# Gate and up products of one request group in Strassen's way, in a two-group FFN on one core

## The chip, the cores and the metric

The kernel runs on one core of one Trainium2 chip, as one launch. The metric is the device time of a run in microseconds (us); lower is better. Three runs of the kernel before gave 1458.1, 1460.4 and 1462.01 us, so the median is 1460.4 us.

The engines are called by the profile's names: PE multiplies matrices (PEld loads its weights), DVE and POOL do element-wise work, ACT evaluates functions and copies, and SP issues the transfers. Each engine works through its own queue in order. PE writes its sums to the PSUM banks; the other operands lie in SBUF.

## The reference, cut to what matters

One encoder layer is computed for a prompt of 1024 frames and a sample of 32 frames, with the same weights. A mixing half (three kinds of heads, an output projection and a first norm) comes first. The change lies in the second half, the feed-forward part, with 1024 model columns and 2816 hidden ones:

```
h = x * (1 + sc2) + sh2
y = (jax.nn.silu(h @ w_gate) * (h @ w_up)) @ w_down
x = _layer_norm(ALPHA * x + (1 + g2) * y, ln2_g, ln2_b)
```

All inputs and outputs are float32.

## The kernel before, in words

**Layout and precision.** Activations are held transposed: 128 model columns on the partitions, frames along the row. The 1056 frames are two groups: group 0 is the first 512 frames, group 1 the other 544 (512 of the prompt and the 32 of the sample). Each group is cut in two column ranges (`MM`, L27), for group 1 of 272 frames each. A float32 operand is split in two parts that PE takes at full rate: a rounded `hi` (ACT, L102 for weights) and the rest `lo` = x - hi (DVE, L103). `gemm` (L108 to L116) makes each product of three matmuls: hi by hi (L114), hi by lo (L115), lo by hi (L116). With 8 blocks of 128 model columns, one product of a 128-column weight tile with one column range is 24 matmuls.

**Weights.** `weights` (L91) loads 128x1024 values (512 KB) into a buffer `raw` (3 of them, `RAW`), and splits them into `whi` and `wlo` (3 of each, `WB`). `w_gu` holds the 1024x128 gate tile and the 1024x128 up tile of hidden tile j as units 2j and 2j+1.

**up** (L965 to L983) makes one tile of 128 hidden units for one group: for each column range a gate product into a PSUM bank of pool `pg` and an up product into one of pool `pu` (3 banks each for group 1), silu as three ACT activations (exp, ln, exp, L977 to L979), two DVE multiplications (L980, L981), and a split into `acth` (ACT, L982) and `actl` (DVE, L983), of which 5 tiles are kept. One tile of group 1 is 4 products or 96 matmuls.

**down** (L999) multiplies 3 or 4 such tiles (`GROUPS`, L29) with `w_down` and adds the result to the residual `z` from PSUM (DVE, L918, in `sublayer_end`). For group 1 the order is: up tiles 0 to 3, down of tiles 0 to 2, up 4 to 6, down, up 7 to 10, down, up 11 to 14, down, up 15 to 18, down. Each `down` stands behind the up of the first tile of the next set. Tiles 19 to 21, their down and group 1's second norm end the kernel (L1218 to L1234).

**Second norm of group 0.** `ln2` (L1013) takes the sums over `z` of group 0 that POOL and DVE made during the last down of group 0 (L835, L844 to L847, L915), makes mean and variance with PE (L854, L856), and then scales and shifts 8 blocks in each of two column ranges: DVE multiplies (L1021), DVE or POOL adds (L1022, "vpvvpvvp": three of eight on POOL), ACT applies gain and bias (L1024), and SP stores to `o_yT`. It is emitted behind up tiles 0 to 3 of group 1 (L1213 to L1215).

**What sets the order.** The program is written with a tile framework. It allots each tile a buffer of its pool and tag, makes an instruction wait until the buffer's last readers are done, and orders each engine's queue by a list schedule in which the place in the program is the priority. The buffers of `z` of group 0 (16 KB on each partition, tag `z0` of pool `pz`) come free when `ln2` of group 0 has been stored; those of the operand of group 0 (`ah0`, `ah256`, `al0`, `al256` of pool `ph`) when its last up tile is done.

The loop in question, before:

```
for g, (j0, nj) in enumerate(GROUPS[:-1]):
    for j in range(j0 + (g > 0), j0 + nj + 1):
        self.up(1, j, act, pa, MM[1])
    if g == 0:
        for a, b in LN[0]:
            self.ln2(0, st, a, b, "vpvvpvvp", "aaaaaaaa")
    st = self.ln_begin(nc.gpsimd, sum=False) if g == last - 1 else None
    self.down(1, g, act, MM[1], st)
```

Of the kernel before, what the change touches and what calls it, by code (L numbers as in the profile page):

```python
# [7 lines left out]
F32 = mybir.dt.float32  # L8
F32R = mybir.dt.float32r
AF = mybir.ActivationFunctionType  # L10
ALU = mybir.AluOpType
# [4 lines left out]
P = 128  # L16
D = 1024
KT = 8
S = 1024
T = 1056  # L20
# [4 lines left out]
GN = (512, 544)  # L25
QD = 2
MM = (((0, 256), (256, 512)), ((0, 272), (272, 544)))  # L27
LN = MM
# [17 lines left out]
FP = (0, 0)  # L46
RAW = 3
WB = 3
ALPHA = 2.0 ** 0.25
LN_EPS = 1e-5  # L50
HN_EPS = 1e-6
# [12 lines left out]
def f(ap):  # L64
    return ap.bitcast(F32)


class Kernel:
# [22 lines left out]
    def weights(self, src, nk, ncol, eng=None):  # L91
# [4 lines left out]
        for k0 in range(0, nk, step):  # L96
            w = step * ncol
            raw = self.t(self.wp, [P, 1056], F32, "raw", RAW)
            self.load(raw[:, :w], src[:, k0 * ncol:k0 * ncol + w])
            hi = self.t(self.wp, [P, 1056], F32R, "whi", WB)  # L100
            lo = self.t(self.wp, [P, 1056], F32R, "wlo", WB)
            nc.scalar.copy(hi[:, :w], raw[:, :w])  # L102
# [16 lines left out]
    def constants(self):  # L119
# [68 lines left out]
    def ada_end(self, u, po):  # L188
# [776 lines left out]
    def up(self, c, j, act, pool, cuts):  # L965
        self.phase = f"up{c}"
        nc, hh, hl = self.nc, self.hh[c], self.hl[c]
        ah, al = act[j] = [self.t(pool, [P, GN[c]], F32R, x, 5) for x in ("acth", "actl")]
        w = [self.weights(self.d["w_gu"][2 * j + i], KT, P) for i in range(2)]
        for a, b in cuts:  # L970
            ps = []
            for i in range(2):
                p = self.t((self.pg, self.pu)[i], [P, 512], F32, self.utag[i])[:, :b - a]
                self.gemm(p, w[i], slice(0, P), lambda k: hh[a][:, k], lambda k: hl[a][:, k])
                ps.append(p)
            s = self.t(self.p2, [P, 272], F32, "sil", 4)[:, :b - a]
            nc.scalar.activation(s, ps[0], AF.Exp, scale=-1.0)  # L977
            nc.scalar.activation(s, s, AF.Ln, bias=self.one)
            nc.scalar.activation(s, s, AF.Exp, scale=-1.0)  # L979
            nc.vector.tensor_tensor(s, ps[0], s, ALU.mult)  # L980
            nc.vector.tensor_tensor(s, ps[1], s, ALU.mult)  # L981
            nc.scalar.copy(ah[:, a:b], s)  # L982
            nc.vector.tensor_tensor(al[:, a:b], s, f(ah[:, a:b]), ALU.subtract)  # L983

    def last_weights(self, dst, units):

        nc = self.nc
        j0, nj = GROUPS[-1]
        w = nj * 256
        out = {}  # L990
        for i, (hi, lo) in zip(units, dst):
            raw = self.t(self.wp, [P, 1056], F32, "raw", RAW)
            self.load(raw[:, :w], self.d["w_dn"][i][:, j0 * 256:(j0 + nj) * 256])
            nc.scalar.copy(hi, raw[:, :w])
            (nc.gpsimd if LWE else nc.vector).tensor_tensor(lo, raw[:, :w], f(hi), ALU.subtract)
            out[i] = [(hi[:, k * 256:(k + 1) * 256], lo[:, k * 256:(k + 1) * 256]) for k in range(nj)]
        return out
# [43 lines left out]
    def run(self):  # L1041
        nc, tc, d = self.nc, self.tc, self.d
        dr = self.pool("dr", space=DRAM)
        t = lambda shape, tag: self.t(dr, shape, F32, tag)
# [14 lines left out]
        s3 = ExitStack()  # L1059
# [15 lines left out]
        w2, w3 = d["w_in"], d["w_in_f"]  # L1075
# [88 lines left out]
        st = self.ln_begin(nc.gpsimd)  # L1164
# [14 lines left out]
        pa = self.pool("pa0", ctx=s5)  # L1179
        self.pu, self.utag = self.pg, "gg"  # L1180
        act = {}
# [27 lines left out]
        act = {}  # L1209
        for g, (j0, nj) in enumerate(GROUPS[:-1]):  # L1210
# [128 lines left out]
```

## Time and profile before

| what | us |
|---|---|
| median of 3 runs | 1460.4 |
| lowest and highest run | 1458.1, 1462.01 |
| the profiled execution | 1461.59 |
| its span, first to last instruction | 1459.8 |
| PE busy, PEld busy | 1396.7, 1345.1 |
| DVE busy, ACT busy, POOL busy | 964.8, 627.2, 283.8 |

The profiled execution is one run of its own; 1.8 us of it lie outside the span. Its tables give, for a group of like instructions, the source line, the engine, the operation, `out<-in` by tile names and shapes, the count, the busy time and the mean of one in ns, and behind the bar the time that the engine stood idle ahead of them and who ended that. Tile names keep the phase in which the buffer was first named, so `wo_ah` is the FFN operand of group 1, `wo_z` its residual and `mlstm_z` that of group 0. Times in windows and timelines count from the start of the span. Group 1's up tiles begin at about 1040 us.

### The profile page before, as it was taken

How to read it: one execution, taken by the hardware profiler on the slowest of the kernel's cores; microseconds unless marked ns; L12 is line 12 of the kernel's file. 1: busy time of each engine (PE TensorE's matmuls, PEld its weight loads, DVE VectorE, ACT ScalarE, POOL GpSimd, SP SyncE). 2: the span in 40 equal slices, each digit the busy share in tenths (PEclk: the TensorE clock that was granted, in tenths of full speed). 3: DMA queues.
4: the chain of work that ended last, by engine and by line, in shares of the span. 5: the costliest groups of instructions: out<-in, count | busy, mean ns of one | idle time of the engine just before them, and what ended most of it. 6: DMA issues, size and time to landing. Idle time of an engine off the chain costs nothing.

```text
span 1459.8 us, 28886 instructions
## 1 busy us (share of the span) xinstructions
PE 1396.7 (96%) x11141; PEld 1345.1 (92%) x11141; DVE 964.8 (66%) x2220; ACT 627.2 (43%) x1365; POOL 283.8 (19%) x335
## 2 busy tenths in 40 slices
PE   7999999999999899999999998998999999999995
PEld 4899988989898799999999998998999999999994
DVE  5558655678698677787877755677648545454676
ACT  3223244534453454555454542334445342424353
POOL 0104100143187300000000000647601000000433
PEclk9999999999999999999999998999999999999997
DMA  9754768563754755444433535321224322222331
GB/s 361 260 194 126 221 199 243 194 197 121 250 188 144 204 166 151 126 125 139 130 111 108 101 94 136 109 86 59 87 73 137 110 87 87 88 88 87 124 108 62
DMA packets 120865, 207.33 MB, mean 142 GB/s; under 512 B 21380, under 2 KB 76300, under 8 KB 120728
## 3 DMA queue, kind: packets, MB, share of 16 engines
q1 hardware_dynamic: 120728, 205.49, 44.8%
q8 instruction: 88, 1.44, 0.4%
q14 instruction: 49, 0.40, 0.1%
HBM read 173.78 MB, written 31.66 MB: 141 GB/s over the span
## 4 chain that ended last, share of the span: by engine, by line
PE 80%; DMA 6%; DVE 6%; POOL 3%; issue 2%; ACT 1%; SPq 1%; DVEq 0%; ACTq 0%; POOLq 0%
PE up_g L115 7%; PE up_g L116 7%; PE up_g L114 7%; PE dn_g L114 4%; PE dn_g L115 4%; PE dn_g L116 4%; PE up_u L116 3%; PE up_u L115 3%; PE up_u L114 3%; PE tm_g L279 3%; PE tm_g L280 3%; PE tm_g L281 3%; PE fox_t L729 2%; PE wo_g L116 2%; PE wo_g L115 2%
## 5 line engine op out<-in xcount | busy, mean ns | idle before, releaser
L114 PE MATMUL up_g<-wo_ah,up_whi 128*128 128x256 f32 (+1 forms) x1056 | 304.1, 289 | 13.2 <-DVE up_sil L980 5.6
L115 PE MATMUL up_g<-wo_al,up_whi 128*128 128x256 f32 (+1 forms) x1056 | 305.3, 289 | 0.1
L116 PE MATMUL up_g<-wo_ah,up_wlo 128*128 128x256 f32 (+1 forms) x1056 | 304.6, 289 | 0.0
L114 PEld LDWEIGHTS up_g<-wo_ah,up_whi 128*128 128x128 f32 x1056 | 201.9, 191 | 16.5 <-DVE up_sil L980 6.0
L115 PEld LDWEIGHTS up_g<-wo_al,up_whi 128*128 128x128 f32 x1056 | 202.1, 191 | 1.4 <-DVE wo_al L938 0.7
L116 PEld LDWEIGHTS up_g<-wo_ah,up_wlo 128*128 128x128 f32 x1056 | 201.7, 191 | 0.7 <-DVE up_wlo L103 0.4
L103 DVE TENSOR_TENSOR up_wlo<-up_raw,up_whi 128x1024 fp32r<-128x1024 f32 x94 | 120.8, 1285 | 68.5 <-ACT up_whi L102 68.2
L102 ACT CAST up_whi<-up_raw 128x1024 fp32r<-128x1024 f32 x94 | 98.5, 1048 | 142.3 <-PE dn_u L115 53.9
L114 PE MATMUL dn_g<-up_acth,dn_whi 128*128 128x256 f32 (+1 forms) x496 | 146.7, 296 | 9.5 <-DVE mlstm_z L918 6.4
L115 PE MATMUL dn_g<-up_actl,dn_whi 128*128 128x256 f32 (+1 forms) x496 | 144.4, 291 | 0.0
L116 PE MATMUL dn_g<-up_acth,dn_wlo 128*128 128x256 f32 (+1 forms) x496 | 143.8, 290 | 0.0
L280 PE MATMUL tm_g<-tm_wlo,start_h1h 128*128 128x256 f32 (+1 forms) x384 | 110.8, 289 | 0.0
L281 PE MATMUL tm_g<-tm_whi,start_h1l 128*128 128x256 f32 (+1 forms) x384 | 110.4, 288 | 0.0
L279 PE MATMUL tm_g<-tm_whi,start_h1h 128*128 128x256 f32 (+1 forms) x384 | 109.8, 287 | 0.2 <-ACT tm_mixs L630 0.2
L114 PE MATMUL fm_g<-start_h1h,fm_whi 128*128 128x256 f32 (+2 forms) x344 | 102.0, 302 | 6.1 <-DVE fm_qkl L364 2.2
L114 PEld LDWEIGHTS dn_g<-up_acth,dn_whi 128*128 128x128 f32 x496 | 96.7, 195 | 11.5 <-DVE mlstm_z L918 7.5
L115 PE MATMUL fm_g<-start_h1l,fm_whi 128*128 128x256 f32 (+2 forms) x344 | 101.8, 296 | 0.2 <-DVE start_h1l L220 0.2
L116 PE MATMUL up_u<-wo_ah,up_wlo 128*128 128x272 f32 x352 | 101.9, 290 | 0.0
L114 PE MATMUL up_u<-wo_ah,up_whi 128*128 128x272 f32 x352 | 101.2, 288 | 0.0
L115 PE MATMUL up_u<-wo_al,up_whi 128*128 128x272 f32 x352 | 101.0, 287 | 0.0
L116 PE MATMUL fm_g<-start_h1h,fm_wlo 128*128 128x256 f32 (+2 forms) x344 | 100.8, 294 | 0.0
L115 PEld LDWEIGHTS dn_g<-up_actl,dn_whi 128*128 128x128 f32 x496 | 96.9, 195 | 0.3
(458 smaller groups left out, 3758.9 us busy)
## 6 DMA issues: line engine op xcount, KB each, us to landing
up_raw<-w_gu SPq DMA_DIRECT2D x94, 512.0 KB
dn_raw<-w_dn SPq DMA_DIRECT2D x30, 512.0 KB
ada_late<-w_ada SPq DMA_DIRECT2D x24, 512.0 KB
wo_raw<-w_o SPq DMA_DIRECT2D x24, 512.0 KB
ada_araw<-w_ada SPq DMA_DIRECT2D x16, 512.0 KB
fm_raw<-w_in_f SPq DMA_DIRECT2D x16, 512.0 KB
tm_raw<-w_in SPq DMA_DIRECT2D x12, 512.0 KB
dn_raw<-w_dn SPq DMA_DIRECT2D x16, 384.0 KB
```

The lines of the kernel that those rows point to most:

```text
L102: nc.scalar.copy(hi[:, :w], raw[:, :w])
L103: (eng or nc.vector).tensor_tensor(lo[:, :w], raw[:, :w], f(hi[:, :w]), ALU.subtract)
L114: nc.tensor.matmul(ps, hi, xh(k), start=start and k == 0, stop=False)
L115: nc.tensor.matmul(ps, hi, xl(k), start=False, stop=False)
L116: nc.tensor.matmul(ps, lo, xh(k), start=False, stop=stop and k == n - 1)
L279: nc.tensor.matmul(ps[:, :ncol], xh, hi, start=k == 0, stop=False)
L280: nc.tensor.matmul(ps[:, :ncol], xh, lo, start=False, stop=False)
L281: nc.tensor.matmul(ps[:, :ncol], xl, hi, start=False, stop=k == 7)
L729: nc.tensor.transpose(ps[:, y * P:(y + 1) * P], probs[y][:, b * P:(b + 1) * P], self.ident)
```

## The change

Tiles 5 to 18 of group 1 (`SJ = 5`; 14 of 22) are made by a new function `sup` in place of `up`. Tiles 0 to 4 and 19 to 21 stay. A tile's four products form a 2x2 block problem: the weight is cut in gate and up, and along the model columns in a lower and an upper half of 4 blocks each; the operand is cut in its two column ranges and the same halves. That is eight block products of 12 matmuls; Strassen's scheme in Winograd's form makes them from seven:

- `sup_operand`, emitted behind tile 2, makes four combinations T of the operand blocks on POOL, 10 additions or subtractions of 128x272 for each of 4 blocks, and splits each into hi and lo (ACT copy, DVE subtraction). They take the buffers of group 0's operand.
- `sup` makes four combinations of each tile's weights on POOL (128x512 each, three of them in place in the raw buffers), and splits 1024 + 1024 + 512 + 1024 columns in place of 1024 + 1024. `w3` has one buffer and `w4` two, all in the memory of group 0's `z0` (`sup_begin`).
- The seven products go to `pu` and `pg` in turn and are added up on the way out of PSUM: two ACT copies and five DVE additions that read PSUM, two POOL additions, and the multiplication of silu on POOL. For even tiles the gate's raw weights have a buffer `sraw` of their own.

The first emission of `ln2` for group 0 moves from behind tile 3 to behind tile 1. The operand buffers are given with 272 columns for either group.

```diff
     def operand(self, c, pool):
-        self.hh[c], self.hl[c] = ({a: self.t(pool, [P, KT, b - a], F32R, f"{x}{a}", 1) for a, b in MM[c]}
-                                  for x in ("ah", "al"))
+        new = lambda tag, n: self.t(pool, [P, KT * 272], F32R, tag, 1)[:, :KT * n].rearrange("p (k n) -> p k n", k=KT)
+        self.hh[c], self.hl[c] = ({a: new(f"{x}{a}", b - a) for a, b in MM[c]} for x in ("ah", "al"))
...
+    def sup_operand(self):
...
+        eng = nc.gpsimd
+        for k in range(4):
+            b = [[(f(hh[t][:, i]), f(hl[t][:, i])) for t in (0, 272)] for i in (k, k + 4)]
+            new = lambda: self.t(self.p2, [P, 272], F32, "tmp", 4)
+            def split(i, x):
+                nc.scalar.copy(self.T[i][0][:, k], x)
+                nc.vector.tensor_tensor(self.T[i][1][:, k], x, f(self.T[i][0][:, k]), ALU.subtract)
+            def diff(x, y):
+                u, v = new(), new()
+                eng.tensor_tensor(u, x[0], y[0], ALU.subtract)
+                eng.tensor_tensor(v, x[1], y[1], ALU.subtract)
+                eng.tensor_tensor(u, u, v, ALU.add)
+                return u
+            split(0, diff(b[0][1], b[0][0]))
+            t3 = diff(b[1][1], b[0][1])
+            split(2, t3)
+            t2 = new()
+            eng.tensor_tensor(t2, t3, b[0][0][0], ALU.add)
+            eng.tensor_tensor(t2, t2, b[0][0][1], ALU.add)
+            split(1, t2)
+            t4 = new()
+            eng.tensor_tensor(t4, b[1][0][0], t2, ALU.subtract)
+            eng.tensor_tensor(t4, t4, b[1][0][1], ALU.add)
+            split(3, t4)
+    def sup_begin(self):
+        x = self.t(self.pz, [P, 4096], F32R, "z0", 1)
+        self.w3 = x[:, 0:1024], x[:, 1024:2048]
+        self.w4 = [(x[:, i:i + 512], x[:, i + 512:i + 1024]) for i in (2048, 3072)]
+    def sup(self, j, act, pool):
...
+        eng = nc.gpsimd
+        split(*w1, rg)
+        eng.tensor_tensor(s3, rg[:, lo], ru[:, lo], ALU.subtract)
+        eng.tensor_tensor(ru[:, lo], ru[:, lo], ru[:, hi], ALU.add)
+        split(*w2, ru)
+        eng.tensor_tensor(rg[:, lo], ru[:, lo], rg[:, lo], ALU.subtract)
+        eng.tensor_tensor(rg[:, hi], rg[:, hi], rg[:, lo], ALU.subtract)
+        split(*w4, s3)
+        split(*self.w3, rg)
...
+        nc.scalar.copy(u2, prod(blocks(w1, 0), own(0, 0)))
+        add(nc.vector, x0, prod(blocks(w1, 512), own(0, 4)), u2)
+        g0 = silu(x0)
+        nc.scalar.copy(c5, prod(blocks(w2, 0), com(0)))
+        add(nc.vector, u2, prod(blocks(self.w3, 0), com(1)), u2)
+        add(eng, x1, u2, c5)
+        add(nc.vector, x1, prod(blocks(self.w3, 512), own(272, 4)), x1)
+        g1 = silu(x1)
+        add(nc.vector, u3, prod(blocks(w4, 0), com(2)), u2)
+        add(eng, c5, u3, c5)
+        end(g1, c5, slice(272, 544))
+        add(nc.vector, u3, prod(blocks(w2, 512), com(3)), u3)
+        end(g0, u3, slice(0, 272))
...
             for j in range(j0 + (g > 0), j0 + nj + 1):
-                self.up(1, j, act, pa, MM[1])
-            if g == 0:
-                for a, b in LN[0]:
-                    self.ln2(0, st, a, b, "vpvvpvvp", "aaaaaaaa")
+                if j == SJ:
+                    self.sup_begin()
+                if j < SJ:
+                    self.up(1, j, act, pa, MM[1])
+                else:
+                    self.sup(j, act, pa)
+                if j == 1:
+                    for a, b in LN[0]:
+                        self.ln2(0, st, a, b, "vpvvpvvp", "aaaaaaaa")
+                if j == 2:
+                    self.sup_operand()
```

Here `silu(x)` is exp, ln, exp on ACT and a multiplication on POOL, and `end` is a DVE multiplication, an ACT copy to `acth` and a DVE subtraction to `actl`.

More of the change, by code (lines that the diff above doesn't have):

```diff
@@ L48 @@
 WB = 3
+SJ = 5
 ALPHA = 2.0 ** 0.25
@@ new lines, in sup_begin, with split, prod, silu @@
+    def sup_begin(self):
[3 more added lines that the diff above has]
+    def sup(self, j, act, pool):
+        self.phase = "sup"
+        nc = self.nc
+        hh, hl, T = self.hh[1], self.hl[1], self.T
+        ah, al = act[j] = [self.t(pool, [P, GN[1]], F32R, x, 5) for x in ("acth", "actl")]
+        if j % 2:
+            rg = self.t(self.wp, [P, 1056], F32, "raw", RAW)[:, :1024]
+        else:
+            rg = self.t(self.px, [P, 1024], F32, "sraw", 1)
+        ru = self.t(self.wp, [P, 1056], F32, "raw", RAW)[:, :1024]
+        self.load(rg, self.d["w_gu"][2 * j])
+        self.load(ru, self.d["w_gu"][2 * j + 1])
+        def split(hi, lo, x):
+            nc.scalar.copy(hi, x)
+            nc.vector.tensor_tensor(lo, x, f(hi), ALU.subtract)
+        w1, w2 = ([self.t(self.wp, [P, 1056], F32R, x, WB)[:, :1024] for x in ("whi", "wlo")] for _ in range(2))
+        lo, hi = slice(0, 512), slice(512, 1024)
+        s3 = self.t(self.px, [P, 512], F32, "s3", 1)
+        w4 = self.w4[j % 2]
+        eng = nc.gpsimd
[7 more added lines that the diff above has]
+        split(*self.w3, rg)
+        blocks = lambda w, c: [(w[0][:, c + k * P:c + k * P + P], w[1][:, c + k * P:c + k * P + P]) for k in range(4)]
+        whole = slice(0, P)
+        def prod(ps, w, x, start=True, stop=False):
+            self.gemm(ps, w, whole, *x, start=start, stop=stop)
+        own = lambda t, k0: (lambda k: hh[t][:, k0 + k], lambda k: hl[t][:, k0 + k])
+        com = lambda i: (lambda k: T[i][0][:, k], lambda k: T[i][1][:, k])
+        n = [0]
+        def prod(w, x):
+            n[0] += 1
+            ps = self.t((self.pg, self.pu)[n[0] % 2], [P, 512], F32, "gu"[n[0] % 2])[:, :272]
+            self.gemm(ps, w, whole, *x)
+            return ps
+        c = lambda p, tag: self.t(p, [P, 272], F32, tag, 4)
+        add = lambda e, o, x, y: e.tensor_tensor(o, x, y, ALU.add)
+        def silu(x):
+            s = c(self.p2, "sil")
+            nc.scalar.activation(s, x, AF.Exp, scale=-1.0)
+            nc.scalar.activation(s, s, AF.Ln, bias=self.one)
+            nc.scalar.activation(s, s, AF.Exp, scale=-1.0)
+            eng.tensor_tensor(s, x, s, ALU.mult)
+            return s
+        def end(s, x, sl):
+            nc.vector.tensor_tensor(s, x, s, ALU.mult)
+            nc.scalar.copy(ah[:, sl], s)
+            nc.vector.tensor_tensor(al[:, sl], s, f(ah[:, sl]), ALU.subtract)
+        u2 = c(self.px, "c")
+        nc.scalar.copy(u2, prod(blocks(w1, 0), own(0, 0)))
+        x0 = c(self.p2, "tmp")
+        add(nc.vector, x0, prod(blocks(w1, 512), own(0, 4)), u2)
+        g0 = silu(x0)
+        c5 = c(self.px, "c")
+        nc.scalar.copy(c5, prod(blocks(w2, 0), com(0)))
+        add(nc.vector, u2, prod(blocks(self.w3, 0), com(1)), u2)
+        x1 = c(self.p2, "tmp")
+        add(eng, x1, u2, c5)
+        add(nc.vector, x1, prod(blocks(self.w3, 512), own(272, 4)), x1)
+        g1 = silu(x1)
+        u3 = c(self.p2, "sil")
+        add(nc.vector, u3, prod(blocks(w4, 0), com(2)), u2)
[3 more added lines that the diff above has]
+        end(g0, u3, slice(0, 272))
```

9 lines of the change are left out of this document (added).

## The prediction

> **What bounds the kernel now.** I read the page first, then the windows of the stretch that the change touches.
>
> ```profile
> span 1459.8 us, 28886 instructions
> PE 1396.7 (96%) x11141; PEld 1345.1 (92%) x11141; DVE 964.8 (66%) x2220; ACT 627.2 (43%) x1365; POOL 283.8 (19%) x335
> PE 80%; DMA 6%; DVE 6%; POOL 3%; issue 2%; ACT 1%; SPq 1%; DVEq 0%; ACTq 0%; POOLq 0%
> ```
>
> ```profile
> core 0: us, PE busy (x) PEld busy (x) DVE busy (x) ACT busy (x) POOL busy (x), PEclk, DMA share, GB/s
> 1040.00:1088.00 48.00, 48.00 (x385) 47.95 (x384) 21.51 (x35) 22.18 (x42) 4.20 (x5) 1.00 0.23 69
> 1088.00:1108.00 20.00, 20.00 (x157) 19.84 (x156) 19.38 (x46) 10.79 (x20) 2.44 (x3) 1.00 0.45 153
> 1144.00:1162.00 18.00, 18.00 (x145) 18.00 (x144) 12.78 (x29) 3.95 (x6) 0.00 (x0) 1.00 0.38 136
> 1162.00:1306.00 144.00, 144.00 (x1151) 144.00 (x1151) 67.00 (x120) 51.57 (x88) 0.00 (x0) 1.00 0.27 89
> 1306.00:1354.00 48.00, 48.00 (x385) 48.00 (x385) 19.89 (x32) 21.45 (x39) 0.00 (x0) 1.00 0.24 77
> ```
>
> PE is the chain (80%), and from 1040 to 1354 it never rests, at full clock: 1306 to 1354 is four up tiles, 384 matmuls in 48.0 us, 12.0 us a tile. That is 48.0/385 = 0.1247 us a matmul. The second window holds group 0's norm and most of the first down; DVE is full there (19.38 of 20), yet PE doesn't wait. So in this stretch a matmul less is 0.125 us less, provided that the other engines still feed PE. POOL is empty from 1144 on. The end of the kernel is not touched.
>
> **The change part by part.**
>
> *Removed from PE.* Seven products of 12 matmuls for eight: 12 x 0.1247 = 1.50 us a tile, 10.5 us for 12.0, and **20.9 us** over 14 tiles.
>
> *Added elsewhere.* Durations of before, from the groups of lines of DVE and ACT (1162 to 1282) and from timelines of POOL and DVE:
>
> ```profile
> L103 DVE TENSOR_TENSOR up_wlo<-up_raw,up_whi 128x1024 fp32r<-128x1024 f32 x14 | 17.2, 1226 | 18.9 <-ACT up_whi L102 18.9
> L981 DVE TENSOR_TENSOR up_sil<-up_u,up_sil 128x272 f32<-128x272 f32 x16 | 7.1, 442 | 11.2 <-PE up_u L116 11.2
> L102 ACT CAST up_whi<-up_raw 128x1024 fp32r<-128x1024 f32 x14 | 14.7, 1049 | 32.8 <-PE dn_u L115 18.4 <-PE up_g L115 11.9 <-PE up_u L115 2.6
> L978 ACT ACTIVATE up_sil<-up_sil,start_ones 128x272 f32<-128x272 f32 x16 | 8.4, 523 | 0.5
> L979 ACT ACTIVATE up_sil<-up_sil 128x272 f32<-128x272 f32 x16 | 6.9, 432 | 0.5
> L977 ACT ACTIVATE up_sil<-up_g 128x272 f32<-128x272 f32 x16 | 6.3, 396 | 14.7 <-PE up_g L116 14.7
> L982 ACT CAST up_acth<-up_sil 128x272 fp32r<-128x272 f32 x15 | 6.3, 417 | 16.5 <-DVE up_sil L981 16.5
> ```
>
> ```profile
> 1024.39 0.72 POOL L845 TENSOR_TENSOR lna_zs<-mlstm_z 128x256 f32<-128x256 f32 x1
> 1030.70 1.70 POOL L845 TENSOR_TENSOR lna_zs<-lna_zs,mlstm_z 128x256 f32<-128x256 f32 x1
> 1032.37 0.92 POOL L845 TENSOR_TENSOR lna_zs<-mlstm_z 128x256 f32<-128x256 f32 x1
> ...
> 1039.44 4.76 POOL L845 TENSOR_TENSOR lna_zs<-lna_zs,mlstm_z 128x256 f32<-128x256 f32 x5
> ...
> 1358.14 2.37 POOL L995 TENSOR_TENSOR dn_z<-dn_raw,dn_z 128x1024 fp32r<-128x1024 f32 x1 [242.08 <-ACT dn_z L994]
> ```
>
> ```profile
> 1030.06 1.76 DVE L103 TENSOR_TENSOR up_wlo<-up_raw,up_whi 128x1024 fp32r<-128x1024 f32 x1
> 1031.75 0.47 DVE L918 SCALAR_TENSOR_TENSOR mlstm_z<-dn_g,start_mod,mlstm_z 128x256 f32<-128x256 f32 x1
> 1032.14 0.55 DVE L847 TENSOR_TENSOR lna_qs<-lna_qs,dn_tmp 128x256 f32<-128x256 f32 x1
> ```
>
> POOL takes 0.72 us for 256 columns and 2.37 for 1024, so by the slope between them 0.75 for 272 and 1.27 for 512 (no row has 512; its ends are 0.72 and 2.37). DVE in the same way takes 0.69 for 512, ACT 0.62. A `sup` tile then costs:
>
> - POOL: 4 x 1.27 + 4 x 0.75 = 8.1 us, where it had none.
> - DVE: splits 3 x 1.226 + 0.69 = 4.4, ends 4 x 0.44 = 1.8, additions from PSUM 5 x 0.44 = 2.2: 8.4 us.
> - ACT: casts 3 x 1.049 + 0.62, two copies of 0.40 (as L977, which reads PSUM too), six activations 2.70, two casts 0.83: 8.1 us.
>
> Each is below PE's 10.5. But POOL and DVE are not independent, and that is where the change is decided. At 1030.06 DVE's 1024 subtraction took 1.76 in place of 1.23, and the POOL operation started in it took 1.70 in place of 0.72. At 1032.14 a 256 addition of DVE (two operands in SBUF) cost POOL 0.92 - 0.72 = 0.20. L918, which reads PSUM, isn't stretched. So the two take turns when DVE reads two SBUF operands; a 1024 subtraction costs POOL 0.98, a 272 operation 0.20, a 512 one by the slope 0.46. In POOL's time a tile is then 8.1 + 3 x 0.98 + 0.46 + 4 x 0.20 = **12.3 us**, against PE's 10.5.
>
> The Trainium skill, SBUF — State Buffer, "Who interferes with whom", says that a VectorE instruction with two SBUF inputs and a GpSimd instruction that reads SBUF exclude each other for the whole of an instruction. The rows agree on the turns, but not that nothing overlaps: 0.20 for an operation of 0.42. By the rule a tile would be 8.1 + 6.2 = 14.3 us; this is the third rival below.
>
> *Sets of four tiles (three of them).* Turns are needed in 4 x 12.3 = 49 us, PE has 42 us of ups and 24 of down, in which only four splits of down's weights (4 x 0.98) use the turns. So there is room over the whole set, and the question is how much can be moved into down. In the order of the changed build's queues, before the first tile of a set its own weights are done (4 x 1.27 + 3.4 = 8.5), and of the second tile two combinations and the small split (3.0); the last tile's results (4 x 0.75 + 0.8 = 3.8) and some 1 us of the tile before trail into down. Left are 49 - 8.5 - 3.0 - 4.8 = 33 us before the last tile's fourth product at 31.5 + 4.5 = 36 us. It fits by 3, less idle turns: POOL's and DVE's queues are in order, so POOL's `x1` stands behind the next tiles' combinations, and DVE's additions from PSUM wait behind it, while PE may run about five products ahead of them (6 banks). I take 1 us of waiting a set: **3 us** (ends: 0, and 5 a set, if each hand-over finds the other queue waiting). Tiles 5 and 6 are two only, with the same lead: nothing.
>
> *The start.* This is the dearest part.
>
> ```profile
> 1087.72 0.43 PE lnb_t L854 x2
> ```
>
> ```profile
> L1021 DVE TENSOR_TENSOR mlstm_z<-mlstm_z,lna_pv 128x256 f32<-128x256 f32 x8 | 3.8, 551 | 0.0
> L103 DVE TENSOR_TENSOR dn_wlo<-dn_raw,dn_whi 128x768 fp32r<-128x768 f32 x2 | 1.9, 952 | 0.3 <-ACT dn_whi L102 0.3
> ```
>
> Group 0's statistics stand behind tile 3, at 1087.7; they move two tiles ahead, to 1063.7. `sup_operand` shares the four buffers `tmp` with them, so it gets going about 5 us later, at 1069. Then POOL has 38 operations of 0.75, six of the norm of 0.72 and two combinations of tile 5, 35.4 us, and DVE takes turns with some 26 operations of the norm, 16 splits and 7 others at 0.20, and 4 splits of 768 and 4 of 1024 columns (3.0 and 3.9): 16.7. That is 52 us, T is ready at 1121. Tile 5 begins at 1087.7 + 1.7 (four statistics matmuls) + 18 (down) + 12 (tile 4) = 1119.4, and wants T at its third product, 1122.4: just in time. Its `w3` comes later: four more combinations on POOL (5.1), two DVE splits between them, and ACT and DVE for `w3` itself (2.3), 1129.5, against the fourth product at 1123.9. I take **5 us** of waiting. Ends: nothing, if POOL is less held, and 13 if splits in DVE's queue, which now stand between the additions of the first down, hold these back as well.
>
> *The rest.* `ln2` stores 2 MB earlier, on SP ahead of loads that are issued early anyway; the loads keep their number and the DMA share is 0.24. The buffer `sraw` is filled first long before, ahead of loads of group 1's output projection, and POOL's two splits of the last weights (2.37 each) now wait for `w3` and `w4` to be read: **1 us** for both (0 to 3). The norm's old place gains nothing, since PE didn't wait there.
>
> *Sum.* -20.9 + 3 + 5 + 1 = **-12 us**.
>
> **The rivals.**
>
> 1. *All of it is hidden.* For it: DVE, ACT and POOL are each below PE's 10.5 us. Against it: the turns, 12.3. Then 1461.6 - 20.9 = 1441, and up to 1445.
> 2. *The start costs 13 or more.* DVE waits for POOL's T in front of the first down's additions, and PE soon has no bank. For it: 52 us of turns in a stretch of 53. Against it: six banks are some 6.8 us of down. -20.9 + 15 + 3 + 1 = -2: 1460, no change.
> 3. *Slower: turns for whole instructions.* Place: the same two stretches. Start: 35.4 of POOL and, at full durations, 49 x 0.43 + 4 x 0.95 + 4 x 1.23 = 30 of DVE, 13 us more than I counted, so 18 of waiting. Sets: a tile is 8.1 of POOL, 4.4 and 1.8 of DVE, 14.3; ahead of a set lie 4 x 1.27 + 4.4 = 9.5 of its first tile and 2 x 1.27 + 0.69 = 3.2 of its second, behind it 4 x 0.75 + 1.8 + 1 = 5.8. 4 x 14.3 - 9.5 - 3.2 - 5.8 = 38.7 against 36, with idle turns some 3 us each at the least; where POOL's results stand behind combinations whose raw buffers are not free yet, no lead is kept, and a set loses up to 4 x (14.3 - 10.5) = 15. -20.9 + 18 + 9 + 1 = +7: 1469, or more. It decides as soon as the waits pass 20.9 us, which is start 12 and 3 a set. For it: DVE 1.76 and POOL 1.70 in one meeting. Against it: 0.20 for 0.42.
> 4. *It doesn't do what it says.* PE's queue in the build has the 168 matmuls less, so only a slower matmul could do it; nothing speaks for that. 1461.
>
> **How the numbers follow.** Forecast (waits of 5 to 14 us, 1447 to 1456) 0.42, all hidden 0.15, the dear start 0.15, slower 0.25, not done 0.03. The likeliest is 1461.6 - 12, **1450 us**, against the profiled execution's own 1461.59; the median of the runs, 1460.4, lies 1.2 lower, which the range takes in. The range goes to 1441 below and, for most of the third rival, to 1470 above. A difference under 0.3% (4.4 us) can't be told from no change here. So faster 0.57 (forecast and all hidden), same 0.18 (dear start, not done), slower 0.25.
>
> **What would show it.** Right: a steady up tile of 10.5 us on PE; POOL at about 80% in the ups with operations of 512 at 1.3 to 2 us; PE's waits in tile 5 for `w3`, on DVE or ACT, of about 5 us, and small ones in the last tile of each set, behind DVE's additions. Rival 1: PE without a wait from 1040 to 1340. Rival 2: waits inside the first down for DVE's L918. Rival 3: POOL and DVE rows that add up with no overlap, and waits in each set of 3 us and more. Wrong altogether: a matmul of more than 0.125 us in `sup`, waits for raw loads, or waits far from this stretch.

## The result, and the profile after

The changed kernel takes 1467.16 us (median of 5 runs, 1463.47 to 1468.98) against 1460.4 before: a ratio of 1.0038 (95% interval 1.0022 to 1.0053). It is slower, where 1450 and a gain were forecast. The profiled execution, from the page and from the windows that were shown of before:

```profile
span 1465.4 us, 28958 instructions
PE 1381.9 (94%) x10973; PEld 1327.7 (91%) x10973; DVE 1050.8 (72%) x2306; ACT 659.1 (45%) x1437; POOL 459.5 (31%) x487
PE 59%; DVE 14%; DMA 8%; POOL 8%; issue 5%; ACT 3%; SPq 1%; DVEq 0%; POOLq 0%; ACTq 0%
```

```profile
1040.00:1088.00 48.00, 48.00 (x381) 47.79 (x380) 33.08 (x54) 26.73 (x55) 20.13 (x22) 1.00 0.30 93
1088.00:1108.00 20.00, 14.08 (x81) 13.54 (x80) 20.00 (x35) 9.98 (x22) 15.87 (x18) 0.72 0.31 96
1144.00:1162.00 18.00, 18.00 (x145) 18.00 (x144) 13.57 (x28) 9.15 (x19) 6.24 (x8) 1.00 0.35 117
1162.00:1306.00 144.00, 140.25 (x1109) 139.31 (x1108) 112.04 (x174) 69.90 (x123) 86.78 (x70) 1.00 0.28 92
1306.00:1354.00 48.00, 45.94 (x365) 45.72 (x364) 37.11 (x48) 26.31 (x48) 27.01 (x23) 1.00 0.27 85
```

The 168 matmuls are gone (11141 to 10973) and PE's busy time is less, but the chain is no longer PE's alone: DVE, DMA and POOL hold 30% of it. In the second window, where before PE made 157 matmuls at clock 1.00, it makes 81, and the granted clock is 0.72. PE's waits between 1030 and 1440 us say where:

```profile
PE sup_u L115 <- DVE sup_tmp L1078: 4.6, 2, 2.5
PE dn_g L116 <- DVE up_actl L984: 4.0, 1, 4.0
PE dn_t L834 <- DVE wo_z L919: 2.1, 1, 2.1
PE dn_g L115 <- DVE up_sil L981: 1.9, 1, 1.9
PE sup_g L117 <- DVE up_z L1046: 1.1, 1, 1.1
PE dn_g L115 <- DVE mlstm_z L919: 0.9, 1, 0.9
PE sup_u L117 <- DVE sup_wlo L1046: 0.7, 1, 0.7
```

Before there was only the row for `mlstm_z`. Two stand in the first down (4.0 and 1.9), two in the sets (4.6, 1.1), one in the last full down (2.1). I compare by the **stretch** from the first matmul of group 0's last down (1008.0 before) to the first of up tile 19 (1379.1): 371.1 us before, 374.1 after, +3.0. Its parts: the ups 0 to 4 and the first down until the first matmul of tile 5, 78.8 before and 90.0 after, **+11.2** (the first 135 matmuls of that down, by which I compare it below, take 18.2 before and 28.3 after); then, each from the start of its first matmul to the end of its last, tiles 5 and 6, 22.2 after against 21.3 where nothing waits (experiment 3), so 0.9 lost; the three sets 44.6, 45.2 and 44.7 against 42.4, so **7.3** lost; the last full down 29.2 against 25.2, **4.0** lost. 11.2 + 0.9 + 7.3 + 4.0 are 23.4 against a saving of 20.5 (14 tiles of 1.47 us). Of the other 2.6 us of the profiled difference 2.4 lie ahead of the stretch. There the profiles of all the kernels below differ by -1 to +7 us from before's, mostly from 290 us on, long ahead of any edit, so I judge by the stretch and by the ratios.

### The profile page after: what moved, and what is told of

Its sections match the earlier page's. It is cut to its first block, busy times and chain, and to the rows that moved or that the text cites. A ratio compares the mean times of both kernels' runs of the same rounds, so it can differ in the third digit from the quotient of the medians.

```text
span 1465.4 us, 28958 instructions
## 1 busy us (share of the span) xinstructions
PE 1381.9 (94%) x10973; PEld 1327.7 (91%) x10973; DVE 1050.8 (72%) x2306; ACT 659.1 (45%) x1437; POOL 459.5 (31%) x487
## 4 chain that ended last, share of the span: by engine, by line
PE 59%; DVE 14%; DMA 8%; POOL 8%; issue 5%; ACT 3%; SPq 1%; DVEq 0%; POOLq 0%; ACTq 0%
PE up_g L116 5%; PE up_g L115 5%; PE up_g L117 5%; PE dn_g L115 3%; PE dn_g L116 3%; PE dn_g L117 3%; PE tm_g L280 3%; PE tm_g L281 3%; PE tm_g L282 3%; PE fox_t L730 2%; PE fm_g L115 2%; PE fm_g L117 2%; PE fm_g L116 2%; PE wo_g L116 2%; PE wo_g L115 2%
## 5 line engine op out<-in xcount | busy, mean ns | idle before, releaser
L115 PE MATMUL up_g<-wo_ah,up_whi 128*128 128x256 f32 (+1 forms) x832 | 240.2, 290 | 11.7 <-DVE up_sil L981 5.6
L116 PE MATMUL up_g<-wo_al,up_whi 128*128 128x256 f32 (+1 forms) x832 | 241.1, 290 | 0.1
L117 PE MATMUL up_g<-wo_ah,up_wlo 128*128 128x256 f32 (+1 forms) x832 | 239.7, 288 | 0.3 <-DVE up_wlo L104 0.3
L115 PEld LDWEIGHTS up_g<-wo_ah,up_whi 128*128 128x128 f32 x832 | 159.5, 192 | 15.2 <-DVE up_sil L981 6.1
L116 PEld LDWEIGHTS up_g<-wo_al,up_whi 128*128 128x128 f32 x832 | 159.8, 192 | 1.5 <-DVE wo_al L939 0.7
L117 PEld LDWEIGHTS up_g<-wo_ah,up_wlo 128*128 128x128 f32 x832 | 159.8, 192 | 0.9 <-DVE up_wlo L104 0.5
L116 PE MATMUL dn_g<-up_actl,dn_whi 128*128 128x256 f32 (+1 forms) x392 | 114.5, 292 | 4.0 <-DVE up_actl L984 4.0
L117 PE MATMUL dn_g<-up_acth,dn_wlo 128*128 128x256 f32 (+1 forms) x392 | 113.7, 290 | 0.0
L104 DVE TENSOR_TENSOR up_wlo<-up_raw,up_whi 128x1024 fp32r<-128x1024 f32 x66 | 86.9, 1316 | 30.1 <-ACT up_whi L103 29.3
L733 ACT CAST fox_pth<-fox_t 128x256 fp32r<-128x256 f32 (+3 forms) x144 | 51.0, 373 | 67.8 <-PE fox_t L730 63.5
```

Source lines behind the costliest of these rows:

```text
L104: (eng or nc.vector).tensor_tensor(lo[:, :w], raw[:, :w], f(hi[:, :w]), ALU.subtract)
L115: nc.tensor.matmul(ps, hi, xh(k), start=start and k == 0, stop=False)
L116: nc.tensor.matmul(ps, hi, xl(k), start=False, stop=False)
L117: nc.tensor.matmul(ps, lo, xh(k), start=False, stop=stop and k == n - 1)
L733: nc.scalar.copy(ph[:, lo:nq], ps[:, lo:nq])
```

## The experiments

Each is the changed kernel with the edit shown, unless it says otherwise. The ratio is to the kernel before on the same chip, with its 95% interval; "stretch" is the difference to before's 371.1.

**1. What the parts of the start cost** (`e1_norm_alone`, the kernel before plus the moved norm; `e11_no_T`).

```diff
-            if g == 0:
+                if j == 1:
                     for a, b in LN[0]:
```

> The kernel before with one edit, group 0's second norm emitted behind tile 1. Theory A (the start of the changed kernel is dear because the norm, the 40 operations of sup_operand on POOL and DVE's splits of T meet in the stretch of the first down, and DVE and POOL exclude each other for whole instructions): the norm alone finds DVE busy 21.5 of 48 us, so nothing is late: 1460.4, within 2. Theory B (it is the move of the norm that pushes DVE's work into the first down): about 8 of the 11 us lost there, 1468, and PE waits in the first down for DVE.

Ratio 0.9994 (0.9977 to 1.0011), stretch +0.4. The norm's move alone costs nothing. `e11_no_T` leaves T's additions and splits out:

```diff
-            split(0, diff(b[0][1], b[0][0]))
...
+            for i, (t, q) in enumerate(((272, k), (0, k), (0, k + 4), (272, k + 4))):
+                nc.scalar.copy(self.T[i][0][:, k], f(hh[t][:, q]))
+                nc.scalar.copy(self.T[i][1][:, k], f(hl[t][:, q]))
```

> The changed kernel with T not computed: ACT copies blocks of the operand into T's places, and the 40 additions on POOL and the 16 splits on DVE are left out. This is the price of T in the changed kernel. Theory (T's work costs the start about 11 us, stop and slow clock together): the stretch falls from 341.5 to 331, ratio 0.996. Rival (the norm, moved ahead of the first down, holds DVE in any case): 337 or more, ratio 1.000.

Ratio 0.996 (0.9944 to 0.9976), stretch -7.0: T costs 10.0 us of the changed kernel. Without it those 135 matmuls take 17.1 us (18.2 where the norm's statistics matmuls lie in it, as before). What of T costs was not yet said.

**2. T later, on another engine, in other buffers.** `e2_late`:

```diff
-SJ = 5
+SJ = 7
...
-                if j == 1:
+                if j == 3:
...
-                if j == 2:
+                if j == 4:
                     self.sup_operand()
```

> The changed kernel with the Strassen tiles from 7 on (12 in place of 14), the norm back behind tile 3 and sup_operand behind tile 4. Theory A: the meeting of norm, T and first down is taken apart, so the first down runs as before (19 us, clock 1.00) and the start costs at most 1; the sets keep their 7.7 of waiting and the last down its 4.0: -18.0 + 7.7 + 4.0 + 1 = -5, 1455. Rival (T costs its 11 us wherever it is made, because DVE's 16 splits and POOL's 40 operations hold back whatever down stands beside them): 1465 to 1467.

Ratio 1.0035 (1.0022 to 1.0048), stretch +4.8: my theory fell, and the rival's number came. PE now stopped 5.0 us in the ups (windows of `e2_late`; DVE is full, POOL nearly):

```profile
1112.00:1128.00 16.00, 16.00 (x130) 16.00 (x129) 16.00 (x28) 6.51 (x14) 14.54 (x15) 1.00 0.23 77
1128.00:1134.00 6.00, 1.00 (x7) 0.78 (x7) 6.00 (x8) 5.79 (x12) 5.06 (x6) 0.74 0.13 45
1134.00:1140.00 6.00, 6.00 (x36) 6.00 (x36) 5.90 (x9) 1.90 (x5) 4.41 (x6) 0.69 0.84 229
```

`e4_T_dve` makes T on DVE:

```diff
-        eng = nc.gpsimd
+        eng = nc.vector
         for k in range(4):
```

> The changed kernel with sup_operand's 40 additions on DVE in place of POOL. Theory A: in turns, 40 x 0.75 become 40 x 0.43, so the start loses about half of its 11 us: 1461 to 1463. Rival (DVE is simply full, 20.0 of 20 us in the window of the first down, and 17 us more in its queue come on top): the first down stands longer, 1473 or more.

Ratio 1.0014 (0.9997 to 1.0031), stretch -1.1. The first down took 20.8, not 28.3, but tiles 5 and 6 waited for T (24.2 us). Better by 4, as the turns would have it, but most of the loss stayed. `e5_own_buf` and `e6_spread` give T's intermediate results buffers of their own; the second also cuts T in parts behind tiles 3 to 6, with `SJ = 7`:

```diff
-            new = lambda: self.t(self.p2, [P, 272], F32, "tmp", 4)
+            new = lambda: self.t(self.px, [P, 272], F32, "c", 4)
...
-                if j == 2:
-                    self.sup_operand()
+                if 3 <= j < 7:
+                    self.sup_operand((j - 3,))
```

> The changed kernel with one edit: the intermediate results of sup_operand get four buffers of their own (the four that the Strassen tiles use later) in place of the four that they share with the second norm and the ups. Theory A2 (order and buffers: T's operations hold the shared buffers and stand ahead of the norm in POOL's queue, so the norm's second half falls into the first down): the norm is done before the first down, which then takes 20 us or less at clock 1.00, and the stretch from group 1's ups to the end of its last full down falls from 341.5 to 333: a ratio to before of 0.998. Rival (turns: the 40 operations of POOL and the splits of DVE exclude each other, in whatever order): the first down still stands for 5 us or more, ratio 1.003.

> The changed kernel with Strassen tiles from 7 on (12 tiles), T in buffers of its own and in four parts of 10 POOL operations, one behind each of tiles 3 to 6; the norm stays behind tile 1. Theory A2 (it is the meeting of all the work in one place that costs): start at most 2, sets 7.7, last down 4.0: -18.0 + 13.7 = -4.3, ratio 0.997. Rival (T costs its 10 us wherever it is made): ratio 1.003, and PE waits of 5 us behind DVE in the ups 4 to 6.

Neither helped, and the rivals' numbers came, or more: 1.0054 (1.0033 to 1.0075), stretch +5.9; 1.0052 (1.0035 to 1.007), stretch +7.1. The place in the program didn't hold T back: its inputs are ready early, so with free buffers the list schedule put T's operations ahead of the norm's and the ups' (POOL is busy 24.9 and 24.8 of the 25 us from 1040 to 1065), and PE stopped in tile 2, for the norm's statistics (`e6_spread`, PE's waits):

```profile
PE lnb_t L855 <- DVE lnb_tmp L860: 4.1, 1, 4.1
```

So shared buffers were not the fault; they had held T back. In the changed kernel that shows as a wait of POOL itself (1046 to 1112 us): it had taken T's first two operations at once, and then stood with all that was behind them.

```profile
POOL sup_tmp L1009 <- DVE lna_pv L866: 22.8, 1, 22.8
```

**3. The sets.** `e3_comb_dve`, in all four lines that combine weights:

```diff
-        eng.tensor_tensor(s3, rg[:, lo], ru[:, lo], ALU.subtract)
+        nc.vector.tensor_tensor(s3, rg[:, lo], ru[:, lo], ALU.subtract)
```

> The changed kernel with the four weight combinations of a tile on DVE in place of POOL. Theory A (whole-instruction turns): a tile's operations that exclude each other fall from 8.1 + 6.2 = 14.3 to 3.0 + 6.2 + 2.8 = 12.0 us, so the waits in the sets fall from 7.7 to 3 or less, and the time to about 1462. Rival (what counts is how much DVE has to do, now 8.4 + 2.8 = 11.2 us a tile against PE's 10.5): the waits grow by about 0.7 a tile, 1475.

Ratio 0.9942 (0.9925 to 0.9959), stretch -8.8. That is better than my theory's 1462: sets of 42.4 us with no wait at all, and the last down takes 26.4; the first down stays at 27.0. Giving DVE more to do (11.2 us a tile) made it faster. `e12_silu_dve` does the opposite share, and `e15_x1_dve` one operation of it:

```diff
-            eng.tensor_tensor(s, x, s, ALU.mult)
+            nc.vector.tensor_tensor(s, x, s, ALU.mult)
...
-        add(eng, x1, u2, c5)
+        add(nc.vector, x1, u2, c5)
...
-        add(eng, c5, u3, c5)
+        add(nc.vector, c5, u3, c5)
```

> The changed kernel with silu's multiplications and the two additions of the results on DVE in place of POOL; the weight combinations stay on POOL. Theory (turns, their sum per tile): 4 x 1.27 of POOL and 6.2 + 4 x 0.44 of DVE are 13.1 us against 14.3 before and 12.0 in e3_comb_dve, so about half of the sets' waits go: stretch 338. Rival (the long 512-column combinations are what a DVE operation waits for, and DVE now has more that waits): 341 or more, with sets no shorter than 44.5.

> The changed kernel with one addition of each Strassen tile, x1 = u2 + c5, on DVE in place of POOL. Theory A (sum of the turns): a tile goes from 14.3 to 14.0 us of operations that exclude each other, so the sets stay at 44.5 to 45. Theory C (x1 stands behind the next tiles' long combinations in POOL's queue, and PE's bank behind x1): the sets fall to 42.4 to 43 and the time by about 6 us, ratio 1.000.

`e12_silu_dve`: 0.9972 (0.9951 to 0.9994), stretch -1.7; the sets 42.4, 42.4 and 43.1. The sum of the turns predicted half; nearly all went. (Tiles 5 and 6 got slower, 25.4 for 22.2, so the stretch gains less.) `e15_x1_dve` (only the middle edit): 0.9995 (0.9977 to 1.0012), stretch -0.2; the sets 43.0, 43.5 and 44.1, so 3.9 of the 7.3 us. One addition of 0.75 us a tile is half of the loss, since it stands in the wrong queue; the rest goes with silu's multiplications or with the combinations. In the changed kernel DVE waited six times for this `x1` (DVE's waits, 1165 to 1355 us):

```profile
DVE sup_tmp L1078 <- POOL sup_tmp L1078: 15.5, 6, 5.3
```

In `e15_x1_dve` there is no such row. POOL's and DVE's timelines of the changed kernel show one of these waits, in the second set:

```profile
1246.86 1.35 POOL L1054 TENSOR_TENSOR sup_s<-sup_raw,sup_raw 128x512 f32<-128x512 f32 x1 [8.13 <-DMA sup_raw<-w_gu]
1248.29 1.29 POOL L1055 TENSOR_TENSOR sup_raw<-sup_raw 128x512 f32<-128x512 f32 x1
1249.54 1.28 POOL L1057 TENSOR_TENSOR sup_sraw<-sup_raw,sup_sraw 128x512 f32<-128x512 f32 x1
1250.90 1.29 POOL L1058 TENSOR_TENSOR sup_sraw<-sup_sraw 128x512 f32<-128x512 f32 x1
1252.15 0.77 POOL L1085 TENSOR_TENSOR sup_sil<-sup_tmp,sup_sil 128x272 f32<-128x272 f32 x1
1252.88 0.78 POOL L1078 TENSOR_TENSOR sup_tmp<-sup_c,sup_c 128x272 f32<-128x272 f32 x1
```

```profile
1247.91 0.44 DVE L1078 TENSOR_TENSOR sup_c<-sup_g,sup_c 128x272 f32<-128x272 f32 x1 [0.85 <-PE sup_g L117]
1253.69 0.44 DVE L1078 TENSOR_TENSOR sup_tmp<-sup_u,sup_tmp 128x272 f32<-128x272 f32 x1 [5.34 <-POOL sup_tmp L1078]
```

The last row of POOL is `x1`. Its input `sup_c` is there at 1248.35, but POOL has three more combinations and a multiplication of silu to do first, and DVE stands for 5.34 us with all that is behind. The combinations come so late since POOL had stood 8.13 us for their raw weights, a case that rival 3 names. PE runs ahead of DVE and stops later, from 1265.7 to 1268.5, for a bank that the next tile has filled. DVE's timeline up to there:

```profile
1260.75 1.97 DVE L1046 TENSOR_TENSOR sup_wlo<-sup_raw,sup_whi 128x1024 fp32r<-128x1024 f32 x1
1262.65 2.98 DVE L1091 TENSOR_TENSOR sup_actl<-sup_sil,sup_acth 128x272 fp32r<-128x272 f32 x2
1265.55 0.43 DVE L1078 TENSOR_TENSOR sup_c<-sup_g,sup_c 128x272 f32<-128x272 f32 x1
1266.44 1.62 DVE L1046 TENSOR_TENSOR up_z<-sup_raw,up_z 128x1024 fp32r<-128x1024 f32 x1 [0.46 <-ACT up_z L1045]
1267.98 0.43 DVE L1078 TENSOR_TENSOR sup_tmp<-sup_u,sup_tmp 128x272 f32<-128x272 f32 x1
```

DVE is late by then, and it is stretched beside POOL's next combinations: the two operations on `sup_actl` (L1091) take 2.98 us for 2 x 0.44. The last row frees the bank for which PE stands still; it waits for the next `x1` (1266.22 to 1266.98) and for one more split. So the order of the queues and the turns both have a part in this stop.

`e8_last_dve`, for the last down:

```diff
-        w = self.last_weights(((t[:, 0], t[:, 1]), (t[:, 2], t[:, 3])), (2, 3))
+        w = self.last_weights(((t[:, 0], t[:, 1]), (t[:, 2], t[:, 3])), (2, 3), nc.vector)
```

> The changed kernel with the lo parts of the first two units of the last weights made on DVE in place of POOL. Theory (the 4.0 us lost in the last full down come from POOL's 2.4 us operation, in which DVE's split and the addition behind it have to wait for their turn): that down takes 26.5 us or less in place of 29.1, ratio 1.002. Rival (they come from the late place, behind the last Strassen tile, on whichever engine): 29 us as before, ratio 1.004.

Ratio 1.0031 (1.0012 to 1.005), stretch +4.6, that down 28.2. This tells nothing apart: `e11_no_T`, where nothing of it was changed, has 27.8. With the combinations on DVE it falls to 26.4 to 27.2 in six kernels, but not in `e10_both_dve` and `e17_paced14_norm1` (28.8 and 28.6). Of the 4.0 us in the changed kernel 2.1 are PE's wait for `wo_z`, and 1.7 come from the clock behind it, 0.51 from 1363.1 to 1366.5 us. Why DVE was late with `wo_z` stays open.

**4. Both together, and T in its place.** `e7_spread_dve` is `e6_spread` with the combinations on DVE, `e10_both_dve` is `e3_comb_dve` and `e4_T_dve` in one, and `e9_T_dve_late` has T on DVE in buffers of its own behind tile 4, `SJ = 7`, and the combinations on DVE.

> As e6_spread, and the weight combinations of a Strassen tile on DVE as in e3_comb_dve. If both effects stand by themselves: start at most 2, sets 1, last down 1.3: -18.0 + 4.3 = -13.7, ratio 0.9905. If T costs its 10 us wherever it is made: -5.7, ratio 0.996.

> The changed kernel with both the 40 additions of T and the weight combinations on DVE (e3 and e4 together; 14 tiles). If the two effects add up: 341.5 - 12.4 - 4.1 = 325 for the stretch, ratio 0.991. Rival (DVE then is full in the first down and in tiles 5 and 6, T comes late): 330 or more, ratio 0.995.

> Strassen tiles from 7 on (12 tiles), the norm behind tile 1, T's 40 additions on DVE with buffers of their own, emitted behind tile 4, and the weight combinations on DVE. Theory (POOL's operations for T, ready long before, stand in POOL's and DVE's queues among the norm's and stretch these; DVE alone has room for T's 24 us in the ups 2 to 6, where it is busy about half of the time): no stop of PE over 1 us before tile 7; the stretch from group 1's ups to the end of the last full down is 338.7 - 18 + 3 = 324, ratio 0.990. Rival (T costs its 8 to 10 us wherever and on whichever engine): 331, ratio 0.995.

`e7_spread_dve`: 0.9984 (0.9971 to 0.9998), stretch -4.0, worse than either number; the stop in tile 2 stayed. `e10_both_dve`: 0.9913 (0.9883 to 0.9943), stretch -9.3. Its ratio is that of the sum, but its stretch is only 0.5 us better than that of `e3_comb_dve`: the 6.2 us won in the first down are lost again in tiles 5 and 6 (23.7), in the sets and in the last down (28.8). `e9_T_dve_late`: 0.9951 (0.9933 to 0.9968), stretch -5.7, the rival's number, but for another reason: from tile 0 to the last down PE has no stop of over 1 us, yet the time isn't there. It went ahead of tile 0: T's operations, now on DVE, were taken into group 0's last down, where DVE's additions to `mlstm_z` and PE stood behind them (PE's waits of `e9_T_dve_late`, 1005 to 1055 us; before has 1.9 and 3.0 in these rows):

```profile
PE dn_g L115 <- DVE mlstm_z L919: 6.5, 4, 3.5
PE dn_g L115 <- DVE up_sil L981: 5.2, 1, 5.2
```

So T was to be held back without standing in a queue. `e13_T_paced` gives its intermediate results the buffers of silu, which each up tile takes in turn, and cuts it in four; the norm goes back behind tile 3, `SJ = 7`, combinations on DVE:

```diff
-            new = lambda: self.t(self.p2, [P, 272], F32, "tmp", 4)
+            new = lambda: self.t(self.p2, [P, 272], F32, "sil", 4)
...
-                if j == 2:
-                    self.sup_operand()
+                if j in (0, 1, 2, 5):
+                    self.sup_operand((min(j, 3),))
```

> Strassen tiles from 7 on (12 tiles), the norm behind tile 3 as in the kernel before, weight combinations on DVE, T's additions on DVE in four parts behind tiles 0, 1, 2 and 5, with the intermediate results in the buffers of silu, so that no part can start before its tile. Theory (place in the queues): 1024 to 1090 has 26 us of DVE idle for 18 of T, no stop of PE before tile 7, group 0's last down as before; against before -18.0 + 1.9 (last down) + 1 = -15, ratio 0.990. Rival (T's amount of work costs, wherever): -18 + 10 + 2 = -6, ratio 0.996.

> As e13_T_paced, with 14 Strassen tiles as in the changed kernel; T's third and fourth part both behind tile 2. Theory (place): -20.9 + 1.9 + 1 and some 3 us because DVE is full in the first down, where the norm, the last part of T and the splits for tile 5 meet: -15, ratio 0.990. Rival (amount): -20.9 + 10 + 2 = -9, ratio 0.994.

> The changed kernel with T in parts as in e14_T_paced14 and the norm behind tile 3, but T's additions and the weight combinations on POOL as the change has them. If the place in the queues costs, and not the engine: the start loses 3 in place of 11, the sets and the last down keep their 7.7 and 4.0: -20.9 + 15 = -6, ratio 0.996. If it is POOL and the turns: +3 or more, ratio 1.002.

`e13_T_paced`: **0.9896** (0.9868 to 0.9925), stretch -16.1, as the theory has it. Its windows, over the same times as before's:

```profile
1040.00:1088.00 48.00, 48.00 (x384) 47.92 (x383) 35.39 (x76) 26.07 (x54) 4.26 (x5) 1.00 0.24 70
1088.00:1108.00 20.00, 20.00 (x157) 19.87 (x156) 19.40 (x46) 10.78 (x20) 2.45 (x3) 1.00 0.46 149
1144.00:1162.00 18.00, 18.00 (x145) 18.00 (x145) 16.48 (x35) 5.46 (x8) 0.00 (x0) 1.00 0.27 87
1162.00:1306.00 144.00, 144.00 (x1148) 144.00 (x1147) 119.72 (x208) 76.17 (x134) 34.34 (x35) 1.00 0.31 99
```

PE never rests in these windows, though DVE has 35.4 us in the first window, more than the changed kernel's 33.1. `e14_T_paced14`: 0.9943 (0.9923 to 0.9964), stretch -10.6, near the rival's number but for a reason of its own; `e16_paced_pool`: 1.0000 (0.9984 to 1.0016), stretch +1.2, between its two numbers. In both the first down is undisturbed, but tile 5 stops, for the memory of group 0's residual, which the late norm still holds (`e14_T_paced14`; 5.8 in the other):

```profile
PE sup_g L115 <- ACT up_z L1045: 6.0, 1, 6.0
```

Two kernels for what was left: `e18_paced_T_pool` is `e13_T_paced` with T's additions on POOL again (`eng = nc.gpsimd`), `e17_paced14_norm1` is `e14_T_paced14` with the norm behind tile 1 and T's parts behind tiles 0 to 3.

> e13_T_paced with T's additions on POOL in place of DVE, at the same places. If place alone decides: the ups 0 to 6 and the first down run without a stop, as in e13, ratio 0.990. If POOL and its turns with DVE cost too: waits for DVE of 2 us and more in the ups 0 to 3 or the first down, ratio 0.993 or more.

> As e14_T_paced14 (14 tiles, all on DVE, T in parts in the buffers of silu), but with the norm behind tile 1 and T's four parts behind tiles 0, 1, 2 and 3. If the stop of 6 us and the slow clock behind it in e14 come from the memory that the late norm holds: they go, and the time is 3 us below e13's by the two further tiles, less 1.7 for the norm's matmuls and about 2 for a fuller first down: ratio 0.989. Rival (DVE is full in the first down and holds back its additions, as in e4 and e10): 3 to 4 us lost there and 2 to 3 in tiles 5 and 6, ratio 0.992.

`e18_paced_T_pool`: **0.9887** (0.9867 to 0.9907), stretch -15.7: with T in its place, POOL makes it as well as DVE. `e17_paced14_norm1`: 0.991 (0.9894 to 0.9927), stretch -11.1; the stop in tile 5 is gone, but the first down takes 22.6 for 18.2, in the rival's way, so the two further tiles give nothing. The two versions with 12 tiles and T in its place, `e13_T_paced` and `e18_paced_T_pool`, are the fastest, at about 1447 us where before took 1463 to 1464 on the same chips; their intervals don't tell them apart.

## Why the prediction was wrong

- **PE's saving, -20.9: right (20.5).** A tile without waits takes 42.4 / 4 = 10.6 us (`e3_comb_dve`, `e13_T_paced`), 1.47 less than before's 48.24 / 4.
- **The start, 5 us (ends 0 to 13): wrong, and the step that decided.** It cost 11.2 + 0.9 = 12.1. I summed the turns of POOL and found T "just in time" for tile 5, with the loss at `w3` (whose terms add up to nearly 1130, not 1129.5; that changes little). The loss came a down earlier: PE stood in the first down, first for `up_actl`, from 1093.8 on, and then for `up_sil`, which stood in DVE's queue behind the norm and the splits of T. DVE's timeline of the changed kernel up to the end of the first stop:

```profile
1090.86 5.82 DVE L1148 TENSOR_TENSOR mlstm_z<-mlstm_z,lna_pv 128x256 f32<-128x256 f32 x8
1096.60 0.43 DVE L982 TENSOR_TENSOR up_sil<-up_u,up_sil 128x272 f32<-128x272 f32 x1
1096.95 0.83 DVE L984 TENSOR_TENSOR up_actl<-up_sil,up_acth 128x272 fp32r<-128x272 f32 x1
```

  Without T the same eight multiplications take 2.77 us (`e11_no_T`). That is the place that rival 2 named, which I gave 0.15, but not its way: it had DVE waiting for POOL's T, and from 1086 to 1112 us DVE waited for nobody, it was full. Its sum of 52 us was no bound either: the same 40 operations cost 10 us (`e11_no_T` against the changed kernel) or nothing (`e18_paced_T_pool`, where the ups 0 to 4 and the first down take no longer than before), by where they stand.
- **No term for the clock.** The stop of 4.2 us was followed by half speed:

```profile
1088.00:1093.00 5.00, 5.00 (x42) 5.00 (x41) 5.00 (x11) 1.52 (x4) 4.18 (x6) 1.00 0.16 62
1093.00:1098.00 5.00, 0.99 (x8) 0.78 (x6) 5.00 (x8) 2.51 (x7) 4.28 (x6) 0.89 0.00 0
1098.00:1104.00 6.00, 4.74 (x20) 4.42 (x20) 6.00 (x9) 4.56 (x10) 4.53 (x5) 0.50 0.21 61
1104.00:1110.00 6.00, 5.34 (x23) 5.34 (x24) 6.00 (x14) 2.15 (x6) 4.65 (x6) 0.50 0.92 285
1110.00:1116.00 6.00, 6.00 (x48) 6.00 (x47) 6.00 (x12) 2.13 (x4) 5.17 (x6) 0.95 0.29 94
```

  The first 135 matmuls of that down take 28.3 us, where 135 x 0.125 are 16.9; waits are 5.9 of the difference (4.0 and 1.9), and most of the other 5.5 is the slow clock (23 matmuls in 5.34 us from 1104 on, 0.23 each).
- **The sets, 3 us: the mechanism was named, the size was wrong.** I wrote that POOL's `x1` stands behind the next tiles' combinations and took 1 us a set; it was 2.2, 2.8 and 2.3. `e15_x1_dve` shows this order as the cause of 3.9 of the 7.3 us. For the rest `e12_silu_dve` and `e3_comb_dve` show only that it goes when one or the other part of POOL's work is moved. The sum of the turns, which I had used for the size, gave only half of what `e12_silu_dve` won in the sets.
- **The turns were priced in POOL's time.** I read 0.20 for a meeting from POOL's row and let DVE's own loss go. But PE waits for DVE, and there a short operation loses what POOL's long one still has to run: in the changed kernel (groups of DVE, 1160 to 1350 us) 272 columns cost 0.94 on the mean, where before has 0.44.

```profile
L1091 DVE TENSOR_TENSOR sup_actl<-sup_sil,sup_acth 128x272 fp32r<-128x272 f32 x20 | 18.4, 939 | 0.3
```

  The Trainium skill, SBUF — State Buffer, "Who interferes with whom", calls this an exclusive lock. I had weighed the rule down on the 0.20; these rows agree with the rule (L1091 beside combinations of 512 columns: 2.98 us for two). Rival 3 had that price and nearly the right end, 1469, but it went by the sum of the turns, and `e12_silu_dve` and `e18_paced_T_pool` show that the sum alone does not decide.
- **The rest, 1 us: too small.** The last full down lost 4.0: a wait of 2.1 and the clock behind it, 1.7; what made DVE late there is not known. The norm's early place was rightly costed at nothing (`e1_norm_alone`).

## What to carry to other kernels

When work is moved to an engine that seemed free, look at the order of its queue first and the sum of its times second: a short operation on which PE's bank hangs must not stand behind long ones that can wait. Work whose inputs are ready early goes where the scheduler finds room, not where it is emitted; buffers that come free at the right time hold it back, and a buffer shared with something late holds back everything behind it in the queue. A stop of PE that is long enough for the clock costs more than itself.

## What the runs showed of the hardware that was not expected

**POOL can starve.** In `e4_T_dve` a POOL operation of 256 columns took 5.15 us in place of 0.72. DVE started eleven operations with two SBUF operands meanwhile, back to back, and POOL's ended 0.69 us after DVE had come to one that reads PSUM (L981). From POOL's and DVE's timelines:

```profile
1093.64 5.15 POOL L1149 TENSOR_TENSOR mlstm_z<-mlstm_z,lna_qs 128x256 f32<-128x256 f32 x1 [14.78 <-DVE mlstm_z L1148]
```

```profile
1092.80 2.76 DVE L1148 TENSOR_TENSOR mlstm_z<-mlstm_z,lna_pv 128x256 f32<-128x256 f32 x8
...
1097.74 0.43 DVE L1005 TENSOR_TENSOR sup_ah<-sup_tmp,sup_ah 128x272 fp32r<-128x272 f32 x1
1098.10 0.43 DVE L981 TENSOR_TENSOR up_sil<-up_g,up_sil 128x272 f32<-128x272 f32 x1
```

In the changed kernel it was DVE that lost: its eight multiplications from 1090.86 on took 5.82 us, while the POOL operations beside them took 0.84 to 0.94. What decides who gets the next turn is not shown.

**The clock after a stop.** Stops are counted here from the start of one matmul to the start of the next, less 0.125 us. Those of 4.2 (the changed kernel), 5.2 (`e2_late`) and 6.2 us (`e14_T_paced14`) all brought the granted clock to 0.50. Of the shorter ones in the sets some did and some didn't, at the same length: in the second set PE stopped 2.68 us in the changed kernel and 2.64 in `e8_last_dve`, in the first with no effect, in the second with a slow stretch behind it. In these traces the granted clock changes only on a grid of 3.41 us. Windows on that grid, with the stop and the time after it, in the changed kernel and in `e8_last_dve`:

```profile
1264.18:1267.60 3.42, 1.77 (x15) 1.55 (x13) 2.96 (x3) 2.23 (x3) 2.80 (x3) 1.00 0.37 134
1267.60:1271.01 3.41, 2.54 (x20) 2.54 (x21) 2.90 (x5) 2.77 (x6) 1.50 (x1) 1.00 0.49 153
```

```profile
1273.26:1276.68 3.42, 1.51 (x12) 1.51 (x13) 3.42 (x5) 2.82 (x7) 0.89 (x2) 1.00 0.25 40
1276.68:1280.09 3.41, 3.41 (x18) 3.41 (x17) 2.72 (x5) 1.69 (x5) 3.41 (x4) 0.50 0.28 114
```

In the changed kernel the grid cuts the stop in 1.65 and 0.87 us without PE; in `e8_last_dve` 1.91 us of it lie in one step, and the next step runs at half clock. The other traces fit: between 990 and 1385 us the 20 kernels have 57 steps at full clock with 2.0 us or more without PE, and each is followed by one at half clock; with 1.4 to 2.0 us it is 14 of 30 steps, and with 0.05 to 1.4 us none of 189. That set took 46.65 us in `e8_last_dve`: 42.38 without a wait, 2.64 for the stop, and 1.6 for the slow clock. So a stop of 2 to 3 us may cost 1.6 us more, by where the grid cuts it, which is one source of the scatter from run to run (not tested by itself). The Trainium skill, TensorE: Matmul & The Clock Gate, "What's actually happening", has a clock that is halved after an idle window of about 3.4 us, where the window runs freely. The grid agrees with that; but 1.91 us without PE in a window were enough here, which is less than the page's idle window, and the measurement decides.
